# Output projection of a two-layer hybrid block: the loads of y are moved into strands of their own

## The chip, the cores and the metric

One core of one Trainium2 chip runs the whole program. Its metric is the device time of one execution in microseconds (us). TensorE (PE in the profile; PEld is its loading of weights) multiplies matrices, VectorE (DVE), ScalarE (ACT) and GpSimd (POOL) work on elements, and SyncE (SP) issues the DMAs that move data between device memory and the on-chip buffers. Each engine runs its own list of instructions in order and waits on semaphores for the others. SPq is SyncE's queue of DMA issues.

## The reference, cut to what matters

The reference is two layers of a bidirectional block over 256 context tokens and 1024 latent tokens of width 1024. In each layer four mixers (mLSTM, differential attention, GLA, gated DeltaNet) give 256 columns of y each. The part that is changed here is the end of a layer:

```
yx = jnp.concatenate([o[1] for o in outs], axis=-1)
x = x + gt[:, None, :] * (yx @ w_out[l])
if need_ctx:
    yc = jnp.concatenate([o[0] for o in outs], axis=-1)
    ctx = ctx + gt_c * (yc @ w_out[l])
```

Layer 0 does this for all ten tiles of 128 tokens, layer 1 for the eight latent tiles alone.

## The kernel before, in words

**The planner.** The program is not written in the order in which it runs. Its parts are strands (`Strand`, line 132), each a Python function in a thread of its own, of which one runs at a time. `Issue` (line 141) keeps a clock for each engine and for SyncE's DMAs ("D"), and a table of when each buffer was last written and read. When a strand wants to issue an instruction, `__call__` (line 310) works out from which moment its operands are there (`dep`) and what it will cost. A DMA counts 0.475 us on SyncE's clock (line 369); its data counts as landed 0.65 us after the issue plus its bytes at 360 GB/s behind the transfers before it, plus 1.0 us (lines 392 to 394). `choose` (line 256) then lets the strand go that can start first; of strands that compete for one engine the one with the smaller rank wins (`RANK`, line 34: "first turn" 1, "out turn" 2, "mlstm" 1). `spawn` (line 229) adds a strand, `need` (line 298) parks one until another has called `set` (line 306) with that name. These names order the writing of the program; what the engines really wait for are semaphores on buffers. All of the kernel's instructions carry the line of the planner's call, L406, in the profile, so groups are told apart by tile names.

**Buffers.** `Pool` (line 441) gives tiles by tag with a number of buffers. A new tile in an old buffer waits until that buffer's last readers are through.

**Output projection in two groups.** The 1024 rows of w_out are cut into eight blocks of 128, and y's columns likewise. `out_first` (line 2651) takes blocks 2, 3, 6, 7 (attention and DeltaNet), which are ready early, and writes x plus its share to the buffer xp in device memory. It runs while the end of GLA and the mLSTM are still at work. `outproj` (line 2729) takes blocks 0, 1, 4, 5 (mLSTM and GLA) and adds them to xp. `q_.need((l, "out first"))` (line 2744) sets it behind the first group. The text calls these the first and the second group.

For each tile of tokens a group does the following:

- `out_load` (line 2611) loads the tile of y, 128 x 512 f32 (262,144 bytes), into one of two buffers tagged "y";
- `out_turn` (line 2624) makes four transposes on TensorE into a PSUM tile "tr", a copy by ScalarE and a subtraction by VectorE into yT, the two halves of a split of y; each has two buffers;
- `out_product` (line 2636) makes 12 products of 128 x 512 for each of the two halves of the columns (nh), 24 in all, into a PSUM tile "o" with two buffers;
- VectorE multiplies by the gate row gtb and adds x or the partial sum (`evacs`, line 2692; `finishes`, line 2850), and a DMA stores the result.

Before the change one strand, `turns` (line 2682 and line 2753), does the load and the turn of a tile one behind the other. For tile i it waits until the products of tile i-2 have been issued, loads y, and turns it. The products are in the strand that spawns the others (lines 2717 and 2885). In `finishes` the load of x for tile i+1 needs `(l, "yT", i + 1)` (line 2855), and the gate row is loaded behind it (line 2865); there are two gate rows in layer 0, one for the context tiles and one for the latent tiles. In layer 0 four more strands (`norms`, `late_turns`, `splits`, `loads`, lines 2783 to 2848) norm and transpose the finished rows for layer 1.

In layer 0 the first group's loads of y are issued from 1043.8 to 1155.5 us and the second's from 1193.3 to 1286.5 us, in layer 1 from 2198.6 to 2308.6 and from 2340.0 to 2382.9 us.

Of the kernel before, what the change touches and what calls it, by code (L numbers as in the profile page):

```python
# [33 lines left out]
RANK = {"evac": 2, "weights": 3, "mlstm": 1, "first": 2, "finish": 2, "proj": 4, "qk": 2, "ahead": 1, "behind": 2, "inner": 0, "gla gates": 2, "decays": 1,  # L34
        "states": 0, "att pe": 1, "att norm": 2, "first turn": 1, "out turn": 2, "out": 4, "mod": 0}
# [105 lines left out]
class Issue:  # L141
# [161 lines left out]
                self.give()  # L303
                self.me.wait = None

    def set(self, name):
        self.done.add(name)


    def __call__(self, e, op, fn, a, k):  # L310
# [119 lines left out]
def _build(tc, nc, A, out, root, dbg):  # L430
    q_ = Issue()
# [34 lines left out]
    def mark(label):  # L466
        if q_.me:
            q_.me.label = label

    def dma(dst, src):  # L470
        SP.dma_start(out=dst, in_=src)
# [2120 lines left out]
    def out_factors(L, p):  # L2592

        l = L.l
        lam_init = 0.8 - 0.6 * math.exp(-0.3 * l)
        fac = (0.25, 0.5 * (1.0 - lam_init), 0.5, 0.5)
        wcol = p([128, 8], "wcol")
        for g in range(4):
            V.tensor_scalar(wcol[:, 2 * g:2 * g + 2], pc(l, ("wn", "wn1", "wn2", "wn3")[g], 0, 2), fac[g], None, ALU.mult)
        return wcol  # L2600
# [10 lines left out]
    def out_load(L, t, ks, op):  # L2611

        b = Box()
        b.t, b.v = t, 1 if t < NCT else 0
        b.y = op([128, len(ks), 128], "y", 2)
        if len(ks) == 4:
            a = yd[L.l][128 * t:128 * t + 128, 128 * ks[0]:128 * ks[0] + 256]
            dma(b.y.rearrange("p (g c) e -> p g (c e)", c=2),
                bass.AP(a.tensor, a.offset, [a.ap[0], [128 * (ks[2] - ks[0]), 2], [1, 256]]))
        else:  # L2620
            dma(b.y.rearrange("p g c -> p (g c)"), yd[L.l][128 * t:128 * t + 128, 128 * ks[0]:128 * ks[0] + 128 * len(ks)])
        return b

    def out_turn(b, ks, op, pps):
        n = len(ks)
        b.yT = [op([128, n, 128], f"yT{i}", 2, F32R) for i in range(2)]
        for k0 in range(0, n, 4):
            m = min(4, n - k0)
            pt = pps([128, 512], "tr")
            for i in range(m):  # L2630
                P.transpose(pt[:, 128 * i:128 * i + 128], b.y[:, k0 + i, :], ident)
            pv = pt[:, :128 * m].rearrange("p (a b) -> p a b", b=128)
            S.copy(b.yT[0][:, k0:k0 + m], pv)
            V.tensor_tensor(b.yT[1][:, k0:k0 + m], pv, b.yT[0][:, k0:k0 + m], ALU.subtract)
# [16 lines left out]
    def out_first(L, wp, end):  # L2651


        l, ks = L.l, (2, 3, 6, 7)
        mark(f"{l}out.first")
        q_.need((l, "w", end, 3))
        raws, wo, O = {}, {}, Box()

        def raw(i):
            if i < len(ks):  # L2660
                raws[i] = wp([128, DM], "wr", 2)
                dma(raws[i], A["w_out"][l, 128 * ks[i]:128 * ks[i] + 128, :])
        raw(0)
        raw(1)
        wcol = out_factors(L, wp)
        for i, (k, name) in enumerate(zip(ks, ((l, "block", end - 1), (l, "half", end), (l, "block", end), (l, "ml")))):
            q_.need(name)
            if i == 3:
                q_.need((l, "levels"))
                O.st = ExitStack()  # L2670
                O.p, O.ps = Pool(O.st, "of"), Pool(O.st, "ofps", PSUM)
                wo[k] = out_split(raws.pop(i), wcol[:, k:k + 1], lambda j, nh: O.p([128, 512], f"wo{j}{nh}", dt=F32R))
            else:
                wo[k] = out_split(raws.pop(i), wcol[:, k:k + 1], lambda j, nh: wp([128, 512], f"w{j}", 6, F32R))
            raw(i + 2)
        q_.need((l, "gdn"))
        bs, n = {}, range(len(L.yt))

        def ev(*k):
            return (l, "of", *k)  # L2680

        def turns():
            mark(f"{l}out.first")
            for i in n:
                if i > 1:
                    q_.need(ev("p", i - 2, 1))
                bs[i] = out_load(L, L.yt[i], ks, O.p)
                out_turn(bs[i], ks, O.p, O.ps)
                bs[i].ps = {}
                q_.set(ev("yT", i))  # L2690

        def evacs():
            mark(f"{l}out.first")
            gtb = {}
            xs = {}

            def load(i):
                xs[i] = O.p([128, DM], "st", 2)
                dma(xs[i], xin(l, L.yt[i]))
            load(0)  # L2700
            for i in n:
                if i + 1 < len(n):
                    load(i + 1)
                t = L.yt[i]
                gt = gates_of(L, t, O.p, gtb)
                for nh in range(2):
                    cs = slice(512 * nh, 512 * nh + 512)
                    q_.need(ev("p", i, nh))
                    ps = bs[i].ps[nh]
                    V.tensor_tensor(ps, ps, gt[:, cs], ALU.mult)  # L2710
                    V.tensor_tensor(xs[i][:, cs], ps, xs[i][:, cs], ALU.add)
                    q_.set(ev("e", i, nh))
                dma(xp[l][128 * t:128 * t + 128, :], xs[i])
                q_.set((l, "first", t))
        q_.spawn(RANK["first turn"], turns)
        q_.spawn(RANK["first turn"], evacs)
        for i in n:
            q_.need(ev("yT", i))
            for nh in range(2):
                if i:  # L2720
                    q_.need(ev("e", i - 1, nh))
                ps = bs[i].ps[nh] = O.ps([128, 512], "o", 2)
                out_product(bs[i], wo, ks, ps, nh)
                q_.set(ev("p", i, nh))
        q_.need((l, "first", L.yt[-1]))
        O.st.close()
        q_.set((l, "out first"))

    def outproj(L):

        l, full = L.l, L.full
        mark(f"{l}out")
        two = parts == "magd"
        ks = (0, 1, 4, 5) if two else tuple(range(8))
        with ExitStack() as st:
            wp, op = Pool(st, "wo", side="right"), None
# [8 lines left out]
            op = Pool(st, "op", side="right")  # L2745
            pps = Pool(st, "opps", PSUM, "right")
# [3 lines left out]
            n = len(L.yt)  # L2750
            todo = [None] * n

            def turns():
                mark(f"{l}out.turn")
                for i in range(n):
                    if "m" in parts:
                        q_.need((l, "mlstm", i))
                    if i > 1:
                        q_.need((l, "o", i - 2, 1))
                    todo[i] = out_load(L, L.yt[i], ks, op)  # L2760
                    todo[i].i, todo[i].ps = i, {}
                    out_turn(todo[i], ks, op, pps)
                    q_.set((l, "yT", i))
                q_.set((l, "turns"))

            def place(t):
                g = next(g for g, (t0, n_) in enumerate(GRP) if t0 <= t < t0 + n_)
# [3 lines left out]
            def ev(*k):  # L2771
                return (l, "late", *k)
            xts, parts_, there = {}, {}, set()
# [76 lines left out]
            def finishes():  # L2850
                mark(f"{l}out.fin")

                def load(i):
                    t = L.yt[i]
                    q_.need((l, "yT", i), (l, "first", t))
                    if i > 2 and not end:
                        q_.need(ev("t", i - 3))
                    x = todo[i].x = op([128, DM], "x", 3)
                    dma(x, xp[l][128 * t:128 * t + 128, :])
                load(0)  # L2860
                for i, t in enumerate(L.yt):
                    if i + 1 < n:
                        load(i + 1)
                    b = todo[i]
                    gt = gates_of(L, t, op, gtb)
                    for nh in range(2):
                        cs = slice(512 * nh, 512 * nh + 512)
                        q_.need((l, "o", i, nh))
                        ps = b.ps[nh]
                        V.tensor_tensor(ps, ps, gt[:, cs], ALU.mult)  # L2870
                        V.tensor_tensor(b.x[:, cs], ps, b.x[:, cs], ALU.add)
                        q_.set((l, "fin", i, nh))
                    if last:
                        dma(out[0, 128 * (t - NCT):128 * (t - NCT) + 128, :], b.x)
                    else:
                        dma(x1[t], b.x)
                    q_.set((l, "fins", i))
            q_.spawn(RANK["out turn"], turns)
            q_.spawn(RANK["out turn"], finishes)
            if end:  # L2880
                q_.set((l, "late"))
# [54 lines left out]
```

## Time and profile before

| | |
|---|---|
| median of 3 runs | 2408.47 us (2407.11 to 2413.15) |
| the profiled execution, its own time | 2405.2 us |
| its span, first to last instruction | 2403.3 us |
| TensorE busy / weight loads | 2113.9 us (88%) / 1737.7 us (72%) |
| VectorE, ScalarE, GpSimd busy | 1500.8, 981.6, 834.4 us |
| granted TensorE clock, mean | 0.942 of full speed |
| DMA on SyncE's queue | 331.69 MB, 46.1% of 16 engines |
| loads of y for the output projection | 36 of 256 KB |

Busy time is the time in which an engine runs instructions; the idle time before an instruction is put down to what released it. A row of the timeline merges neighbours of one kind: start, length, engine, operation, output tile <- input tiles, shapes, count, and in brackets the idle time ahead of it with its releaser. An issue on SPq lasts as long as SyncE needs to hand the DMA over; the transfer ends later. A stretch's DMA share is the mean busy share of the 16 DMA engines, worked out from the times of packets, so that a full stretch can read a little over 1. The granted clock is the share of full speed at which TensorE was allowed to run.

### The profile page before, as it was taken

How to read it: one execution, taken by the hardware profiler on the slowest of the kernel's cores; microseconds unless marked ns; L12 is line 12 of the kernel's file. 1: busy time of each engine (PE TensorE's matmuls, PEld its weight loads, DVE VectorE, ACT ScalarE, POOL GpSimd, SP SyncE). 2: the span in 40 equal slices, each digit the busy share in tenths (PEclk: the TensorE clock that was granted, in tenths of full speed). 3: DMA queues.
4: the chain of work that ended last, by engine and by line, in shares of the span. 5: the costliest groups of instructions: out<-in, count | busy, mean ns of one | idle time of the engine just before them, and what ended most of it. 6: DMA issues, size and time to landing. Idle time of an engine off the chain costs nothing. (4 is left out here: it accounts for less than half of the span.)

```text
span 2403.3 us, 57716 instructions
## 1 busy us (share of the span) xinstructions
PE 2113.9 (88%) x23367; PEld 1737.7 (72%) x23367; DVE 1500.8 (62%) x2726; ACT 981.6 (41%) x2168; POOL 834.4 (35%) x1048
## 2 busy tenths in 40 slices
PE   5898999999898998888877888889999889976888
PEld 1656778888776677876765668888788667775776
DVE  3586669555386863537666476696633778655475
ACT  2346412433276763213334264313322667632240
POOL 1244523555122224332431244433433122255240
PEclk7899999999999999989989899999999999986999
DMA  7347643445513116258963236433444431164595
GB/s 264 108 140 233 192 147 102 146 146 161 161 44 93 53 51 166 67 128 252 280 214 114 70 108 189 135 113 100 144 124 125 120 98 35 50 170 99 155 302 184
DMA packets 348053, 335.38 MB, mean 140 GB/s; under 512 B 93147, under 2 KB 292283, under 8 KB 347275
## 3 DMA queue, kind: packets, MB, share of 16 engines
q1 hardware_dynamic: 347786, 331.69, 46.1%
q8 instruction: 185, 3.03, 0.5%
q14 instruction: 82, 0.66, 0.1%
HBM read 226.78 MB, written 107.43 MB: 139 GB/s over the span
## 5 line engine op out<-in xcount | busy, mean ns | idle before, releaser
L406 PE MATMUL mm<-w,hT 128*128 128x256 f32 x4512 | 641.2, 293 | 17.6 <-DVE st L406 10.2
L406 PEld LDWEIGHTS mm<-w,hT 128*128 128x128 f32 x4512 | 576.1, 193 | 50.4 <-issue 20.5
L406 PE MATMUL mm<-hT,w 128*128 128x512 f32 (+1 forms) x1680 | 388.8, 377 | 20.3 <-ACT w L406 5.9
L406 PEld LDWEIGHTS mm<-hT,w 128*128 128x128 f32 x1680 | 283.2, 194 | 91.9 <-issue 20.8
L406 DVE TENSOR_REDUCE st<-sc 128x1 f32<-128x1024 f32 (+1 forms) x200 | 200.0, 1026 | 66.8 <-PE sc L406 65.6
L406 ACT ACTIVATE p<-sc,st 128x256 f32<-128x256 f32 (+1 forms) x272 | 211.3, 786 | 68.3 <-DVE st L406 51.7
L406 POOL TENSOR_TENSOR w<-wr,w 128x512 fp32r<-128x512 f32 x54 | 80.7, 1495 | 275.3 <-ACT w L406 220.9
L406 POOL TENSOR_TENSOR hss<-hss,mhalf 128x2 f32<-128x2 f32 (+2 forms) x72 | 104.1, 1446 | 157.1 <-DVE hss L406 143.1
L406 PE MATMUL o<-wo,yT 128*128 128x512 f32 x540 | 148.9, 412 | 4.8 <-DVE x L406 3.2
L406 PE MATMUL sc<-KT,qt 96*128 96x512 f32 (+1 forms) x400 | 124.2, 400 | 29.8 <-DMA KT<-akh 12.9
L406 ACT COPY wt<-tr 128x512 f32<-128x512 f32 (+1 forms) x200 | 102.2, 511 | 66.0 <-PE tr L406 65.6
L406 ACT COPY st<-mm 128x512 f32<-128x512 f32 (+1 forms) x81 | 44.9, 554 | 204.2 <-PE mm L406 142.0
L406 POOL TENSOR_TENSOR ss<-ss,mhalf 128x1 f32<-128x1 f32 (+1 forms) x39 | 68.4, 1754 | 168.9 <-DVE ss L406 168.7
L406 PEld LDWEIGHTS o<-wo,yT 128*128 128x128 f32 x540 | 102.1, 195 | 29.6 <-DVE x L406 3.8
L406 PE MATMUL tr<-k_ident,p 128*128 128x128 f32 x656 | 115.2, 281 | 7.5 <-ACT wt L406 7.0
L406 POOL TENSOR_TENSOR st<-st 128x1 f32<-128x1 f32 (+1 forms) x136 | 27.1, 199 | 270.8 <-ACT p L406 190.4
L406 ACT CAST w<-wr 128x512 fp32r<-128x512 f32 x128 | 77.4, 622 | 98.0 <-PE mm L406 56.7
L406 PE MATMUL po<-wt,av 128*64 128x128 f32 x1312 | 105.3, 284 | 3.5 <-DVE aacc L406 3.5
L406 PEld LDWEIGHTS sc<-KT,qt 96*128 96x128 f32 x400 | 63.6, 196 | 58.9 <-ACT p L406 30.9
L406 DVE SCALAR_TENSOR_TENSOR p<-p,st,p 128x1280 f32<-128x1280 f32 (+1 forms) x72 | 103.0, 1430 | 2.5 <-POOL st L406 2.3
L406 PE MATMUL o<-w,yT 128*128 128x512 f32 x324 | 100.9, 439 | 4.0 <-DVE st L406 4.0
L406 DVE TENSOR_TENSOR w<-wr,w 128x512 fp32r<-128x512 f32 x74 | 68.1, 922 | 54.5 <-ACT w L406 54.3
(314 smaller groups left out, 4062.8 us busy)
## 6 DMA issues: line engine op xcount, KB each, us to landing
wr<-in_w_in SPq DMA_DIRECT2D x64, 512.0 KB
wm<-in_w_mod SPq DMA_DIRECT2D x64, 256.0 KB
y<-y SPq DMA_DIRECT2D x36, 256.0 KB
xp<-st SPq DMA_DIRECT2D x18, 512.0 KB
pd<-rs_NG SPq DMA_DIRECT2D x18, 512.0 KB
kq<-kq SPq DMA_DIRECT2D x18, 512.0 KB
x<-xp SPq DMA_DIRECT2D x18, 512.0 KB
wm<-in_w_mod SPq DMA_DIRECT2D x16, 512.0 KB
```

The costliest lines, as they stand in the source:

```text
L406: r = fn(*a, **k)
```

## The change

In both groups the load leaves `turns` for a new strand `fetches`, spawned ahead of `turns` with the same rank. `fetches` loads tile i as soon as the transposes of tile i-2 have been issued ("turned"), which are the last readers of its buffer. `turns` waits for the load ("y") and, as before, for the products of tile i-2. In the second group the wait for the mLSTM's tile moves with the load. `set` takes several names, so that one call can set "turned" and "yT".

```diff
-    def set(self, name):
-        self.done.add(name)
+    def set(self, *names):
+        self.done.update(names)
...
         def turns():
             mark(f"{l}out.first")
             for i in n:
+                q_.need(ev("y", i))
                 if i > 1:
                     q_.need(ev("p", i - 2, 1))
+                out_turn(bs[i], ks, O.p, O.ps)
+                q_.set(ev("turned", i), ev("yT", i))
+
+        def fetches():
+            mark(f"{l}out.first")
+            for i in n:
+                if i > 1:
+                    q_.need(ev("turned", i - 2))
                 bs[i] = out_load(L, L.yt[i], ks, O.p)
-                out_turn(bs[i], ks, O.p, O.ps)
                 bs[i].ps = {}
-                q_.set(ev("yT", i))
+                q_.set(ev("y", i))
...
+        q_.spawn(RANK["first turn"], fetches)
         q_.spawn(RANK["first turn"], turns)
...
             def turns():
                 mark(f"{l}out.turn")
                 for i in range(n):
+                    q_.need((l, "y there", i))
+                    if i > 1:
+                        q_.need((l, "o", i - 2, 1))
+                    out_turn(todo[i], ks, op, pps)
+                    q_.set((l, "y turned", i), (l, "yT", i))
+                q_.set((l, "turns"))
+
+            def fetches():
+                mark(f"{l}out.turn")
+                for i in range(n):
                     if "m" in parts:
                         q_.need((l, "mlstm", i))
                     if i > 1:
-                        q_.need((l, "o", i - 2, 1))
+                        q_.need((l, "y turned", i - 2))
                     todo[i] = out_load(L, L.yt[i], ks, op)
                     todo[i].i, todo[i].ps = i, {}
-                    out_turn(todo[i], ks, op, pps)
-                    q_.set((l, "yT", i))
-                q_.set((l, "turns"))
+                    q_.set((l, "y there", i))
...
+            q_.spawn(RANK["out turn"], fetches)
             q_.spawn(RANK["out turn"], turns)
```

## Rows read from the trace of the kernel before

**Rows 1.** The page: busy time of each engine, its share of the span, instructions.

```profile
PE 2113.9 (88%) x23367; PEld 1737.7 (72%) x23367; DVE 1500.8 (62%) x2726; ACT 981.6 (41%) x2168; POOL 834.4 (35%) x1048
```

**Rows 2.** TensorE's waits, 1040–1200, 1190–1300, 2240–2403: us, times, longest.

```profile
PE tr L406 <- DMA y<-y: 4.1, 3, 3.2
...
PE tr L406 <- DMA y<-y: 7.2, 5, 3.2
...
PE tr L406 <- DMA y<-y: 8.5, 4, 5.8
```

**Rows 3.** Busy time by stretch (windows); columns in the first line.

```profile
core 0: us, PE busy (x) PEld busy (x) DVE busy (x) ACT busy (x) POOL busy (x), PEclk, DMA share, GB/s
1193.00:1256.00 63.00, 48.30 (x233) 38.32 (x232) 39.27 (x76) 23.02 (x55) 24.60 (x25) 0.85 0.69 224
1330.00:2198.00 868.00, 780.02 (x9026) 663.09 (x9029) 554.07 (x964) 388.11 (x825) 310.82 (x403) 0.94 0.38 112
2254.00:2340.00 86.00, 72.93 (x604) 62.71 (x594) 57.09 (x120) 31.77 (x97) 36.91 (x45) 0.92 1.02 284
2357.00:2390.00 33.00, 33.00 (x153) 26.73 (x153) 18.38 (x28) 2.93 (x5) 0.00 (x0) 1.00 0.63 214
```

**Rows 4.** Timeline of SyncE's queue, layer 0, second group.

```profile
1223.51 0.85 SPq L406 DMA_DIRECT2D y<-y  x1
...
1230.99 0.82 SPq L406 DMA_DIRECT2D y<-y  x1
1234.21 0.34 SPq L406 DMA_DIRECT2D x<-xp  x1
1234.61 0.45 SPq L406 DMA_DIRECT2D gtb<-gt  x1
```

**Rows 5.** Timeline of TensorE, same stretch: start, us, what, [idle before <-releaser].

```profile
1207.66 0.66 PE L406 MATMUL tr<-k_ident,y 128*128 128x128 f32 x4 [0.96 <-DMA y<-y]
...
1219.21 9.93 PE L406 MATMUL o<-wo,yT 128*128 128x512 f32 x36
...
1233.12 0.63 PE L406 MATMUL tr<-k_ident,y 128*128 128x128 f32 x4 [0.40 <-DMA y<-y]
...
1238.31 0.63 PE L406 MATMUL tr<-k_ident,y 128*128 128x128 f32 x4 [3.19 <-DMA y<-y]
1240.32 1.09 PE L406 MATMUL tr<-k_ident,x 128*128 128x128 f32 x4 [1.38 <-DVE x L406]
1244.01 5.96 PE L406 MATMUL o<-wo,yT 128*128 128x512 f32 x14 [2.61 <-DVE x L406]
```

**Rows 6.** Timeline of TensorE, layer 0, first group, tile 0.

```profile
1046.93 1.12 PE L406 MATMUL tr<-k_ident,y 128*128 128x128 f32 x4 [3.18 <-DMA y<-y]
```

**Rows 7.** Timeline of TensorE, layer 1, both groups.

```profile
2247.90 0.38 PE L406 MATMUL tr<-k_ident,y 128*128 128x128 f32 x2
...
2280.08 1.09 PE L406 MATMUL tr<-k_ident,y 128*128 128x128 f32 x4 [5.78 <-DMA y<-y]
...
2349.52 0.63 PE L406 MATMUL tr<-k_ident,y 128*128 128x128 f32 x4 [1.48 <-DMA y<-y]
...
2355.67 0.63 PE L406 MATMUL tr<-k_ident,y 128*128 128x128 f32 x4 [1.78 <-DVE o L406]
```

**Rows 8.** Timeline of SyncE's queue, layer 1, first group, tiles 3 and 4.

```profile
2253.87 0.53 SPq L406 DMA_DIRECT2D y<-y  x1
...
2274.74 0.56 SPq L406 DMA_DIRECT2D y<-y  x1
```

**Rows 9.** The chain that ended last, layer 1: start, us, what.

```profile
2274.74 5.20 DMA y<-y
...
2347.94 6.91 DMA gtb<-gt
```

**Rows 10.** SyncE's waits, 1040–1200: us in total, times, longest.

```profile
SPq L406 <- DVE st L406: 10.1, 4, 6.0
SPq L406 <- DMA xp<-st: 8.0, 5, 2.3
```


## The prediction, made before the changed kernel was run

> **What bounds the kernel now.** I read the page's busy shares first, then the windows by stretch, then what TensorE waits for, then single loads on the SyncE queue. TensorE is busy for 88% of the span [rows 1], so over the whole run only idle TensorE time can be won, and the question is how much of it is owed to y. For each of the 36 y tiles TensorE makes four transposes and 24 products. It sat idle before transposes of y for 4.1 us in layer 0's first group, 7.2 us in its second group and 8.5 us in both groups of layer 1 [rows 2]. Together that is 19.8 us in 12 waits, 0.8% of the run: a ceiling for what waiting on y costs directly, unless something stands behind a late y as well.
>
> The stretches differ. In the first half of layer 0's second group TensorE is busy 48.30 of 63 us with the DMA engines at 0.69. While layer 1's first group shares the chip with the mLSTM, TensorE is busy 72.93 of 86 us and the DMA share is 1.02: there the transfers themselves press. In layer 1's last stretch TensorE is busy for 33.00 of 33 us, although y is issued there tile by tile too [rows 3]. So nothing is to be had at the very end: one tile's 24 products cover the load there.
>
> **Where y is late.** In layer 0's second group, tile 3's load went out at 1223.51 and tile 4's at 1230.99 [rows 4]; their transposes began at 1233.12 and 1238.31 after idle 0.40 and 3.19 us [rows 5]. From issue to use that is 9.6 and 7.3 us. Tile 4's products are further back: 36 products took 9.93 us [rows 5], so 24 take about 6.6 us. That is less than the load. More hangs on tile 3: line 2855 lets the finishing strand load x for tile 3, and after it the second gate row, only when the planner has seen tile 3's turn. Both went out at 1234.21 and 1234.61 [rows 4], and the products of tile 3 then waited 2.61 us for VectorE's finishing of tile 2 [rows 5].
>
> **The change, part by part.** The number of DMAs, matmuls and copies stays as it is; nothing is added on an engine. What moves is the place of 32 of the 36 loads in SyncE's queue: from behind the second product of tile i-2 to behind the transposes of tile i-2, which is a product of 24 earlier; tile 1's load goes out beside tile 0's. Only the first two loads of a group are free of any wait. The transposes of tile i still wait for the products of tile i-2 (two yT buffers), so they cannot themselves move ahead without limit. `set` taking several names costs the chip nothing: it runs while the program is written.
>
> *Layer 0, the first group.* Of the 4.1 us, 3.18 us stand before tile 0 [rows 6], whose load isn't moved. That leaves 0.9 us. Bounds 0 to -0.9; I take -0.3, since the DMA share of this stage soon comes to that of layer 1.
>
> *Layer 0, the second group.* The five waits of 7.2 us [rows 2] go if y is there: tile 3's load would stand behind the transposes of tile 1 at 1207.66 instead of at 1223.51 [rows 4, 5], some 15 us earlier against 9.6 us of flight. Tile 3 could then turn when tile 1's products end, at about 1219.21 + 24/36 x 9.93 = 1225.8 rather than 1233.12, and x and the gate row would follow up to 7 us earlier, so at best the 2.61 us go too: -9.8. What is late next is VectorE's norm and finish of the tile before: the same stretch has TensorE waiting 1.38 and 2.61 us for it [rows 5]. If such waits return in full (4.0 us), -3.2 is left. I take -5, nearer to the lower end, as VectorE's norms (39.27 us busy of 63 [rows 3]) are not moved.
>
> *Layer 1, the first group.* One wait of 5.78 us, before tile 4, makes up most of it [rows 7]; the four waits of both groups sum to 8.5 us [rows 2], and 1.48 us of those are the second group's [rows 7]. So 7.0 us at best. Tile 3's and tile 4's loads left at 2253.87 and 2274.74 [rows 8]; tile 4's would follow the transposes of tile 2, which end at 2248.3 [rows 7], before the DMA engines fill. The chain that ended last passes through this load for 5.20 us [rows 9]. But the DMA share of 1.02 at 284 GB/s [rows 3] says that after it the mLSTM's own loads set the pace: if so only two loads of 262,144 bytes leave the full stretch, 0.92 us each by that rate, -1.8. Between -1.8 and -7.0 I take -3.5, as the chain turns to other DMAs later.
>
> *Layer 1, the second group.* Tile 1's 1.48 us, then 1.78 us behind the finishing of tile 0 [rows 7], which waited for the gate row (6.91 us on the chain [rows 9]). Bounds 0 to -3.3; I take -1.5, tile 1's wait. Once the dense stretch begins, nothing: the cover is the 24 products of a tile, at 33.00 of 33 us [rows 3].
>
> *The price on SyncE's queue.* At each of four group starts a second load goes ahead of x, the gate row and the mLSTM's loads: 0.53 to 0.85 us of issue [rows 4, 8] and 0.92 us of transfer by the rate above, at most some 1.5 us each or 6 in all; below nothing it cannot be. I take +0.5, because at three of the four starts nothing waits for what follows.
>
> *The planner.* Every strand after 1043 us is re-ordered by the planner's clock, layer 1's middle too. The trace cannot price that; TensorE idles 868 - 780 = 88 us between 1330 and 2198 [rows 3], and I let a twentieth of it come or go: +-4.4, taken as 0.
>
> The sum is -0.3 - 5 - 3.5 - 1.5 + 0.5 = **-9.8 us**, bounds -25.4 to +5.4. It is made against the profiled execution (2405.2 us, span 2403.3), which lies 3.3 us below the median of the three runs shown, 2408.47 us. I carry it over to the median: **2398.7 us**. A measurement of this kernel can tell about 0.3%, 7.2 us, from no change.
>
> A rule against the change: the Trainium skill, "DMA: Bandwidth & Descriptors", section on the anatomy of one DMA, gives (for GpSimd-issued transfers) about 2.0 us fixed plus bytes at 436 GB/s; an estimate from it is 2.6 us for a y tile, which 24 products cover, and the sum would be 0. The measured 7.3 and 9.6 us [rows 4, 5] speak against it here, as SyncE's transfers share full engines, so the rows decide.
>
> **The rivals.** *The DMA engines are the bound* (0.30). Then layer 1's first group gives 1.8, layer 0's second group 3.2, the rest nothing: -5 + 0.5 = -4.5, about **2404 us**. For it speaks the share of 1.02 [rows 3]; against it the 5.78 us hole, in which TensorE stood for this one load [rows 7].
>
> *SyncE blocks on the new waits* (0.14), **slower**. A load that is issued behind transposes waits on SyncE until they have run, and every load of the mLSTM behind it waits along. SyncE now loses 10.1 us in 4 waits for evacuations and 8.0 us in 5 for stores in layer 0's first group [rows 10], 2.0 us each. Nine y loads lie in the two full stretches: 18 us lost, and layer 1's 3.5 us not won: -6.3 + 18 = +11.7, **2420 us**. It decides from about 1.1 us lost for each. Against it: TensorE runs these transposes early, and in full stretches the queue is behind the plan anyway, so that waits have passed. The Trainium skill, the same page and section, says that semaphore waits happen on the issuing sequencer before dispatch; by that rule the blocking is possible, and the waits of rows 10 agree that SyncE waits in order.
>
> *A larger gain* (0.13). TensorE's granted clock averages 0.85 between 1193 and 1256 us [rows 3], so part of it ran at 1.2 instead of 2.4 GHz after idle spells. If the holes close and the stretch runs at 1.00, 48.30 x 0.15 = 7.2 us come on top: -17, **2391.5 us**.
>
> *The change does not do what it says* (0.03): the planner sets the loads where they were. **2408.5 us**.
>
> **How the numbers follow.** The forecast itself, -7.2 to -14 us, has 0.40; its own range is 2394 to 2401. Faster by over 0.3%: 0.40 + 0.13 = 0.53. Within: 0.30 + 0.03 = 0.33. Slower: 0.14. The range goes from 2385 (larger gain with the planner's swing) to 2414 (the bounds' upper end), which leaves out most of the blocking case and the far lower end.
>
> **What would show it.** Right: y waits of TensorE down from 19.8 us to the 3.18 us of tile 0 and little more; layer 0's x load and gate row for tile 3 several us sooner after the group's start; the hole before tile 4 in layer 1 gone; the last dense stretch as long as before. Wrong: SyncE waiting for transposes for over 10 us in the full stretches; or y waits gone and TensorE idle as long, for the mLSTM's loads or VectorE's norms. A swing of over 5 us between 1330 and 2198 would mean that the planner, not the loads, set the result.

## The result, and the profile after

The changed kernel takes 2438.09 us, the median of 3 runs (2436.53 to 2442.72), against 2408.47 us before: ratio 1.0111, 95% interval 1.0069 to 1.0153. It is slower by 1.1% by that ratio, some 27 us (the two medians lie 29.6 us apart), and lies above the range of the prediction. The span of its profiled execution is 2436.3 us, 33.0 us longer than before.

The page's busy shares answer to [rows 1]:

```profile
PE 2130.2 (87%) x23367; PEld 1750.1 (72%) x23367; DVE 1504.5 (62%) x2720; ACT 985.3 (40%) x2169; POOL 833.7 (34%) x1055
```

The same 23367 matmuls keep TensorE busy for 16 us more; the other 17 us of the span are idle time of TensorE. The mean granted clock of the execution is 0.935, and 0.942 before; an estimate from these, 2113.9 x 0.942 / 0.935 = 2129.7 us, is close to the 2130.2 us of busy time, so the 16 us go with the lower clock.

TensorE's waits for y, in layer 0's first group, its second group and layer 1's groups (1040 to 1205, 1200 to 1330, 2200 to 2436 us; us in total, times, longest), answer to [rows 2]:

```profile
PE tr L406 <- DMA y<-y: 2.9, 1, 2.9
...
PE tr L406 <- DMA y<-y: 5.1, 1, 5.1
...
PE tr L406 <- DMA y<-y: 0.8, 1, 0.8
```

They fell from 19.8 us in 12 waits to 8.8 us in 3: the loads are early, as the change means them to be. Layer 1's hole of 5.78 us before tile 4 [rows 7] is gone. And yet the kernel is slower.

Windows set to the stretches of [rows 3] (layer 0's second group, layer 1's middle, the mLSTM with the first group, the dense last stretch; columns as there). The new order has moved matmuls from one to another (406 for 604 in the third line), so the shares can be compared and not the lengths:

```profile
1206.00:1269.00 63.00, 46.04 (x213) 37.98 (x212) 32.98 (x65) 22.40 (x48) 19.58 (x19) 0.78 0.66 211
1343.00:2221.00 878.00, 779.64 (x8917) 662.14 (x8915) 561.15 (x960) 388.06 (x819) 312.32 (x405) 0.94 0.37 111
2301.00:2390.00 89.00, 73.58 (x406) 63.59 (x407) 56.19 (x124) 33.00 (x102) 34.50 (x47) 0.87 0.96 272
2395.00:2428.00 33.00, 33.00 (x153) 26.77 (x152) 18.30 (x28) 2.94 (x5) 0.00 (x0) 1.00 0.59 206
```

The dense last stretch is as it was, 33.00 us of 33. The other stretches are no denser: layer 1's middle, in which no load of y is issued, is busy for 0.89 of its window, where it was 0.90.

To see where the time went, I read four landmarks from SyncE's queue: the first load of y in layer 0, the first load of layer 1's gate weights (graw), the first load of y in layer 1, and the last store of the output; between the last two stands the mLSTM's first load of NG (pd<-rs_NG), which opens its output part. The timeline of the queue, after:

```profile
1044.68 0.57 SPq L406 DMA_DIRECT2D y<-y  x1
...
1330.79 1.64 SPq L406 DMA_DIRECT2D graw<-in_w_in  x3
...
2224.68 1.21 SPq L406 DMA_DIRECT2D y<-y  x2
...
2301.48 0.59 SPq L406 DMA_DIRECT2D pd<-rs_NG  x1
...
2426.64 5.93 SPq L406 DMA_DIRECT2D out<-x  x2
```

Before, the same landmarks stand at 1043.83, 1317.92, 2198.64 and 2394.02 us. In us between them:

| stage | before | after | difference |
|---|---|---|---|
| layer 0's two groups (first y to graw) | 274.1 | 286.1 | +12.0 |
| layer 1's middle (graw to its first y) | 880.7 | 893.9 | +13.2 |
| layer 1's two groups (first y to last store) | 195.4 | 202.0 | +6.6 |

So all stages lose, and the largest part is lost where the change does nothing. Between these landmarks the matmuls are nearly the same, so busy time can be compared; first before, then after:

```profile
1043.83:1317.92 274.09, 219.69 (x1552) 173.92 (x1552) 167.46 (x344) 93.77 (x233) 86.97 (x101) 0.91 0.71 210
1317.92:2198.64 880.72, 785.42 (x9066) 666.84 (x9068) 557.01 (x975) 391.70 (x832) 314.73 (x408) 0.94 0.38 111
2198.64:2394.02 195.38, 165.71 (x1644) 136.47 (x1645) 122.28 (x237) 48.34 (x139) 57.86 (x66) 0.92 0.72 211
```

```profile
1044.68:1330.79 286.11, 226.71 (x1554) 181.68 (x1552) 162.30 (x338) 97.33 (x240) 86.12 (x101) 0.87 0.70 201
1330.79:2224.68 893.89, 787.68 (x9057) 667.80 (x9057) 565.61 (x975) 391.99 (x827) 317.65 (x414) 0.94 0.37 109
2224.68:2426.64 201.96, 171.88 (x1649) 140.54 (x1650) 121.13 (x237) 48.24 (x138) 56.14 (x67) 0.91 0.69 204
```

Of the 31.8 us, 15.4 are busy time of TensorE (7.0, 2.3 and 6.2 us by stage) and 16.3 are idle time (5.0, 10.9 and 0.4 us). The mean granted clock fell most in layer 0's groups, from 0.91 to 0.87. Whether it fell because of new holes between the matmuls is not shown. (Two profiles of one order can differ by 10 us in these stages, as e9 shows below, so the split is rough.)

In layer 1's groups the mLSTM's first load of NG now goes out 76.8 us behind the first load of y, 56.5 us before. Ahead of it stands a wait of the kind that a rival named:

```profile
2240.73 0.41 SPq L406 DMA_DIRECT2D mv<-mv  x1
2256.44 0.53 SPq L406 DMA_DIRECT2D y<-y  x1
2258.38 0.34 SPq L406 DMA_DIRECT2D xp<-st  x1
...
2261.41 0.43 SPq L406 DMA_DIRECT2D kq<-kq  x1
...
2267.64 2.35 SPq L406 DMA_DIRECT2D y<-hy  x4
```

Between 2241.1 and 2256.4 us SyncE waits with tile 3's load until the transposes of tile 1 have read the buffer; the mLSTM's loads kq and GLA's loads gz stand behind it. Whether this wait is what puts the mLSTM back is for e3 to tell. Over the whole run SyncE waits for transposes for 101.9 us (42.7 before):

```profile
SPq L406 <- PE tr L406: 101.9, 28, 15.2
```

Two readings offered themselves: SyncE's blocking (theory queue, later loads), or the new order in which the planner sets everything behind the first changed strand (theory replan, later order).

### The profile page after: what moved, and what is told of

Read it like the earlier page. It is cut to its first block, busy times and chain, and to the rows that moved or that the text cites. A ratio compares the mean times of both kernels' runs of the same rounds, so it can differ in the third digit from the quotient of the medians.

```text
span 2436.3 us, 57725 instructions
## 1 busy us (share of the span) xinstructions
PE 2130.2 (87%) x23367; PEld 1750.1 (72%) x23367; DVE 1504.5 (62%) x2720; ACT 985.3 (40%) x2169; POOL 833.7 (34%) x1055
## 4 chain that ended last, share of the span: by engine, by line
PE 54%; DMA 14%; DVE 11%; issue 7%; ACT 5%; SPq 5%; POOL 3%; POOLq 0%; ACTq 0%; DVEq 0%
PE mm L406 24%; PE po L406 5%; SPq L406 5%; PE o L406 5%; PE tr L406 4%; PE sc L406 3%; PE pd L406 3%; PE p L406 3%; DMA wm<-in_w_mod 2%; DMA wr<-in_w_in 2%; DVE st L406 2%; DMA pd<-rs_NG 2%; PE mod L406 1%; PE puw L406 1%; ACT p L406 1%
## 5 line engine op out<-in xcount | busy, mean ns | idle before, releaser
L406 ACT CAST w<-wr 128x512 fp32r<-128x512 f32 x128 | 76.8, 621 | 104.2 <-DMA wr<-in_w_in 55.2
L406 PEld LDWEIGHTS sc<-KT,qt 96*128 96x128 f32 x400 | 62.9, 195 | 60.2 <-ACT p L406 32.1
L406 PEld LDWEIGHTS tr<-k_ident,p 128*128 128x128 f32 x656 | 75.5, 141 | 35.3 <-ACT wt L406 20.7
```

The costliest lines, as they stand in the source:

```text
L406: r = fn(*a, **k)
```

## The experiments

They ran on four chips (e1 to e4, e5 to e8, e9 to e11 and e12 to e15 on one each), on which the kernel before has medians of 2419 to 2422 us; every ratio is against runs of before beside it on the same chip, with its 95% interval.

**Order and place taken apart.** A DMA's entry in the planner's clock was split from its issue. In e1 the planner counts each load where before had it, so that all four compute engines have exactly the order of before, while the real load is issued behind the transposes of tile i-2 (tiles 0 and 1 at the group's start; in the second group only where the mLSTM's tile is there by then, else at the old place). In e2 it is the other way round: the order of the changed kernel, the loads late.

```diff
+    def out_count(b):          # planner's clock only
+        q_("D", "dma_start", lambda **k: None, (), b.io)
+    def out_issue(b):          # the real DMA, no clock
+        nc.sync.dma_start(**b.io)
...
-                bs[i] = out_load(L, L.yt[i], ks, O.p)
+                out_count(bs[i])
                 out_turn(bs[i], ks, O.p, O.ps)
+                early(i + 2)   # tile and out_issue
```

> The order of every instruction on TensorE, VectorE, ScalarE and GpSimd is that of before; only the loads of y are moved in SyncE's queue, to right behind the transposes of tile i-2. Theory queue (SyncE stands behind a load of y whose buffer is still to be read by transposes, and the loads behind it start late): slower than before by 10 to 35 us, 2418 to 2443 us, with SyncE waiting for transposes for 20 us or more in layer 1's first group, and the mLSTM's first load of NG in layer 1 30 us or more later after the first load of y than the 56.5 us of before. Theory replan (the new order of the other work costs the time, and early loads are good in themselves): 2395 to 2408 us.

e1: 2423.04 us, ratio **1.0011** (0.9994 to 1.0029). Neither theory's number came: early loads in the old order are neither slower nor faster. TensorE's waits for y, over the whole run, are gone; the kernel before, run again on another of these chips (e9, below), has

```profile
PE tr L406 <- DMA y<-y: 23.5, 12, 5.9
```

and e1 has none. SyncE waits for transposes for 62.9 us in e1 (the second line is of the loads issued past the planner, line 2625):

```profile
SPq L406 <- PE tr L406: 37.6, 12, 12.7
...
SPq L2625 <- PE tr L406: 25.3, 10, 7.8
```

against this in e9:

```profile
SPq L406 <- PE tr L406: 41.2, 15, 11.6
```

So 21.7 us more of blocking and 23.5 us less of waiting for y together move the time by no more than 0.3% (7 us). Whether the two cancel is for e4 to tell. What took the place of the waits is in TensorE's waits of layer 1's groups (2200 to 2430 us), first e9, then e1:

```profile
PE tr L406 <- DMA y<-y: 9.3, 4, 5.9
PE m L406 <- ACT cs L406: 8.5, 1, 8.5
...
PE m L406 <- POOL wb L406: 2.4, 2, 1.4
```

```profile
PE m L406 <- ACT cs L406: 8.5, 1, 8.5
PE m L406 <- POOL wb L406: 8.2, 4, 3.3
PE o L406 <- DVE x L406: 4.2, 1, 4.2
```

9.3 us for y went, and 5.8 us more for GpSimd's product with wb and 4.2 us for VectorE's finishing came: TensorE arrives earlier at the next thing that is late.

> The order of every instruction on the four compute engines is that of the changed kernel; only the loads of y go back behind the products of tile i-2, just ahead of the transposes that read them. Theory queue: the blocking is gone, so most of the 30 us is won back: 2403 to 2418 us. Theory replan: the order holds the loss, 2430 to 2450 us.

e2: 2505.37 us, **1.0345** (1.0317 to 1.0373). Neither theory's number came: without the early loads the new order does not win back its loss, it loses more. The run is harsher than its expectation says, and so no clean test of theory queue: this order has the transposes planned right behind the products, and TensorE waits for a late load 22 times:

```profile
PE tr L406 <- DMA y<-y: 70.3, 22, 7.5
```

It tells that the new order rests on early loads, not what the order costs by itself. That is read from e1 against the changed kernel: both have early loads, and 1.0011 against 1.0111 is the new order's, with the blocking that comes with it. The next run takes the blocking out.

**Three buffers.** `b.y = op([128, len(ks), 128], "y", 3)` in the changed kernel. The order of the compute engines stays (in the traces VectorE's differs in 4 of 2720 rows, ScalarE's and GpSimd's in none), the blocking goes.

> The changed kernel with three buffers for y instead of two, so that a load waits for the transposes of tile i-3, which are a tile older. Theory queue: SyncE hardly waits for transposes, 2400 to 2415 us. Theory replan: the order is about that of the changed kernel, 2425 to 2445 us.

e3: 2440.50 us, **1.0083** (1.0061 to 1.0105). SyncE's wait for transposes is down to the level of before,

```profile
SPq L406 <- PE tr L406: 43.5, 16, 11.7
```

and the loss remains. If blocking has a share in the changed kernel's 1.0111, it is some 0.3%, and the intervals overlap. By stage nothing is won:

```profile
1050.93:1336.40 285.47, 225.94 (x1552) 181.47 (x1552) 163.44 (x337) 97.46 (x240) 85.12 (x101) 0.87 0.69 201
1336.40:2229.91 893.51, 789.66 (x9062) 670.79 (x9062) 563.65 (x975) 391.72 (x827) 318.30 (x414) 0.93 0.37 109
2229.91:2432.57 202.66, 173.90 (x1649) 141.84 (x1645) 122.66 (x237) 48.38 (x138) 56.05 (x67) 0.89 0.70 203
```

The three stages are as long as in the changed kernel, within 0.7 us each. In layer 1 SyncE waits for transposes for 3.7 us between the first load of y and the mLSTM's first load of NG (23.4 us in the changed kernel), and still that load goes out 76.9 us behind. So it is the order that puts the mLSTM back, not the blocking.

**One tile ahead in the old order.** As e1, with three buffers, and tile i+1 loaded where before loads tile i.

> Order of the compute engines as before, three buffers for y, and each load where before had the load of the tile ahead of it: one tile early, into a buffer that was read long ago. Theory queue: early loads without the wait, so the 16 us of waits before transposes of y go and something of it is kept: 2395 to 2405 us. Theory replan: the same, 2395 to 2405 us. If it is not faster than before, then the waits for y were covered by others, as the rival says in which the DMA engines set the pace: 2405 to 2412 us.

e4: 2418.93 us, **0.9992** (0.9973 to 1.0010). TensorE's waits for y are down to 0.9 us and SyncE's for transposes are 41.6 us, as in e9; the time is that of before. So the saved waits are worth at most 0.3% by themselves and nothing that was measured, and in e1 there was no gain of that size that the blocking could have eaten: both are covered. This is the mildest form of the change, and no run of this study is clearly faster than the kernel before.

**Is it the mLSTM's place?** Counted in TensorE's order, 72 products of layer 1's first group stand ahead of the mLSTM's first weighing before, 114 after. e5 holds that group back:

```diff
                 if i > 1:
                     q_.need(ev("turned", i - 2))
+                    if l:
+                        q_.need((l, "m states"))   # set behind the mLSTM's last state_out
```

> The changed kernel, with the load of the third and later tiles of layer 1's first group held until the mLSTM's states of that layer have been written. The planned order then has 66 products of that group ahead of the mLSTM's first weighing (before: 72, changed: 114). Theory order (the planner lets the first group's products go ahead of the mLSTM, whose loads fill the DMA engines and set the end): the 20 to 25 us of layer 1's end come back, so +2 to +14 us against before. Theory loads (early loads of y cost in themselves): no change against the changed kernel, +20 to +32 us.

e5: 2458.01 us, **1.0152** (1.0132 to 1.0173). Neither theory's number came. The run is slower still, with 66 products ahead; but in its trace the mLSTM's first load of NG goes out 74.0 us behind the first load of y all the same, so holding the group back did not bring the mLSTM forward, and e5 does not settle the question. e13 and e15 below do.

**Parts of the change.** e6 has the new strands in the second group only, e15 in the first only, e10 in layer 0 only, e11 in layer 1 only.

> The change in the second group only; the first group loads as before, in both layers. The planned order has 120 products of layer 1's first group ahead of the mLSTM's first weighing all the same, since the planner's clock differs from layer 0's second group on. Theory order: +15 to +30 us against before, though that group's loads are not moved. Theory loads: the first group is as before, so within 8 us of before.

> The change in the first group only, in both layers. 1415 rows of TensorE's order differ, 120 products ahead of the mLSTM's first weighing. Theory order: +15 to +35 us, like the whole change and like the second group alone, not a share of it. Theory loads: the two groups share the loss, so +0 to +10 us beside the +25 us of the second group alone.

> The change in layer 0 alone (both groups); layer 1 loads y as before. The planner plans all that follows anew: 1349 rows of TensorE's order differ from before. Theory order: nearly the whole loss is here, +20 to +32 us, of it 8 us or more in layer 1's middle and end, where no load was moved. Theory loads: the part of layer 0 alone, +8 to +14 us, and layer 1 as long as before.

> The change in layer 1 alone. Everything up to layer 1's first group is ordered as before, and behind it the order differs little: 105 rows of TensorE's order. Theory order: within 6 us of before, with most of layer 1's 8.5 us of waits for y gone. Theory loads: the share of layer 1's sixteen tiles, +8 us or more, with SyncE waiting for transposes.

e6: 2446.54 us, **1.0119** (1.0101 to 1.0138). e15: 2429.21 us, **1.0033** (1.0013 to 1.0053). e10: 2454.22 us, **1.0124** (1.0103 to 1.0145). e11: 2425.05 us, **1.0022** (1.0004 to 1.0041). e6 and e11 came as theory order expected, e10 (+35 us) lost more than either theory said. The parts do not add up: the second group alone costs as much as both, layer 0 alone as much as both layers. e11, whose order is nearly that of before, costs almost nothing, although TensorE's waits for y are shorter there too (17.6 us, 23.5 in e9). e15's number (+10 us) lies below what theory order expected and at the upper end of what theory loads did; it has 120 products ahead of the mLSTM, whose first load of NG goes out 81.2 us behind the first load of y, and that this costs so little speaks against the mLSTM's place. Theory loads falls with e6, which was to stay within 8 us, and with the runs that follow.

**A new order with no load moved.** The kernel before, with one line that sets the planner's DMA clock on by a little where layer 0's first group starts:

```diff
         def turns():
             mark(f"{l}out.first")
+            if l == 0:
+                q_.now["D"] += 1.0
```

> The kernel before, with no load moved; only the planner's clock for DMAs is set on by 1.0 us where layer 0's first group starts, so that it plans another order. 115 products stand ahead of the mLSTM's first weighing in layer 1. Theory order: +12 to +30 us against before. Theory loads: no load was moved, so within 6 us of before.

> As the last, with 2.0 us. 93 products stand ahead of the mLSTM's first weighing in layer 1. Theory order: between before and the last, +4 to +16 us. Theory loads: within 6 us of before.

> The kernel before, no load moved, the planner's clock for DMAs set on by 0.05 us where layer 0's first group starts. 1410 rows of TensorE's order differ from before. Theory order at large (any new plan is some per mille longer, since before's order is a good one among many): +15 to +40 us, as with 1 and 2 us. Theory size (a small disturbance gives a small loss): within 5 us of before.

> As the last, with 0.1 us. 900 rows differ, but in layer 1 the first group and the mLSTM stand to each other as before: 72 products ahead of the mLSTM's first weighing. Theory layer 1's end (that place makes the loss): within 5 us of before. Theory order at large: +10 to +40 us.

> As the last two, with 0.5 us: 1583 rows differ, 120 products stand ahead of the mLSTM's first weighing in layer 1. Both theories of the order: +15 to +40 us.

| run | clock set on by | median us | ratio | 95% interval |
|---|---|---|---|---|
| e12 | 0.05 us | 2426.11 | 1.0020 | 1.0001 to 1.0038 |
| e13 | 0.1 us | 2440.18 | 1.0075 | 1.0047 to 1.0104 |
| e14 | 0.5 us | 2440.62 | 1.0081 | 1.0051 to 1.0110 |
| e7 | 1.0 us | 2457.26 | 1.0161 | 1.0142 to 1.0179 |
| e8 | 2.0 us | 2441.80 | 1.0085 | 1.0051 to 1.0119 |

The chip does the same work in these kernels, with the same loads from the same strands; only the plan is another. A plan is the order and, for some copies and products, the choice of the engine, which helpers make by the planner's clocks (`evac`, `sub`, `mulv`, lines 473 to 497): e12 has 2707 instructions on VectorE and 1061 on GpSimd, before 2726 and 1048. They lose 0.2 to 1.6%, and the changed kernel's 1.1% lies in the midst of them. e13 keeps the mLSTM's place (72 products ahead) and loses 0.75%: theory layer 1's end falls. e7 (+36 us) and e8 (+21 us) lost more than was expected of them, and e12 (+7 us) less, so a new order is not always dear. The landmarks show where e13 loses; first e9, then e13:

```profile
1056.56 0.57 SPq L406 DMA_DIRECT2D y<-y  x1
...
1335.90 1.74 SPq L406 DMA_DIRECT2D graw<-in_w_in  x3
...
2219.34 0.56 SPq L406 DMA_DIRECT2D y<-y  x1
...
2417.09 5.94 SPq L406 DMA_DIRECT2D out<-x  x2
```

```profile
1047.50 0.57 SPq L406 DMA_DIRECT2D y<-y  x1
...
1323.89 1.75 SPq L406 DMA_DIRECT2D graw<-in_w_in  x3
...
2231.24 0.55 SPq L406 DMA_DIRECT2D y<-y  x1
...
2429.43 5.94 SPq L406 DMA_DIRECT2D out<-x  x2
```

Layer 0's groups take 279.3 us in e9 and 276.4 in e13, layer 1's groups 197.8 and 198.2, but layer 1's middle 883.4 and 907.4. There e13's matmuls keep TensorE busy for 13.2 us more and leave it idle for 10.7 us more; again first e9, then e13:

```profile
1335.90:2219.34 883.44, 787.07 (x9066) 667.85 (x9068) 558.82 (x975) 391.74 (x832) 312.49 (x408) 0.93 0.38 110
1323.89:2231.24 907.35, 800.26 (x9066) 677.57 (x9068) 548.50 (x973) 391.45 (x830) 320.17 (x412) 0.92 0.37 107
```

The largest single wait of TensorE that e13 has there and e9 has not is for a load of the DeltaNet's gate rows (1330 to 1900 us):

```profile
PE tr L406 <- DMA pk<-rs_BH: 8.4, 1, 8.4
```

Each order loses in places of its own: e10 and e14 lose most in layer 1's groups, which take 211.7 and 214.7 us, 197.8 in e9.

The lower clock is no matter of one profile. Averaged over all runs of a kernel, the granted clock is 0.937 to 0.939 in before and in e1, e4, e9, e11, e12 and e15, whose ratios are at most 1.0033; it is 0.930 to 0.934 in e3, e5 to e8, e10 and e13, whose ratios are 1.0075 to 1.0161, and 0.923 in e2. Only e14 (0.937, 1.0081) stands outside. So in these runs a dear order goes with matmuls that run at a lower clock, beside any longer idle time; which of the two comes first is not shown.

**The kernel before again.**

> The kernel before itself, unchanged: ratio 0.998 to 1.002 by every theory. It gives a trace of before on the chip on which these runs are made, so that the stages can be compared on one chip.

e9: 2422.47 us, **1.0005** (0.9989 to 1.0022), as expected. Its profile is 10 us longer from the first load of y to the last store than the profile of before in [rows 3], though the order is the same (5 us of it busy time of TensorE), so differences of a few us between single profiles say little; the ratios carry the verdicts.

## Why the prediction was wrong, point by point

**The step that failed is the planner's term**, "I let a twentieth of it come or go: +-4.4, taken as 0". The five clock shifts, which move nothing but the plan, measured it: +0.2 to +1.6%, that is +5 to +39 us, never below 0. Nothing in the trace stood behind the twentieth, so a term of up to 39 us was left beside a sum of -9.8, and it was wrongly taken as even to both sides. It was also priced on the wrong thing: on TensorE's idle time in layer 1's middle alone. Of the 31.8 us that the changed kernel's three stages lose, 10.9 are such idle time; 15.4 are the matmuls' own time at a lower granted clock, for which the sum has no term, and 5.4 are idle time in the output projection's own stages. Eleven orders other than that of before were timed (the changed kernel, e5 to e8, e10 to e15), and none was faster. That the order of before is a good one among many is what they suggest; they are too few to say how good. The prediction's own test was right: a swing of over 5 us in layer 1's middle "would mean that the planner, not the loads, set the result", and it was +13.2 (+2.7 in e9, whose order is that of before).

**The gains (-0.3, -5, -3.5, -1.5)** failed as well, in a second way. Each counted a wait of TensorE for y as time won, with a share given back. e1 took all of these waits away, 23.5 us, and the time moved by +0.1% (-0.1 to +0.3). The share given back is the whole: the sum of these terms, by itself, is 0 within 7 us. (The second term also counted on an earlier x and gate row, which e1 does not move; see below for these.) The rival that said so for the full stretches (the DMA engines set the pace) was right about the outcome there; that transfers were the cover is not shown, since what replaced the waits in layer 1 was GpSimd and VectorE. The estimate from the Trainium skill's page "DMA: Bandwidth & Descriptors", anatomy of one DMA, came to a sum of 0 too, but by a load of 2.6 us (its fit is for GpSimd-issued transfers), which the measured loads of 7.3 and 9.6 us [rows 4, 5] contradict.

**SyncE blocks on the new waits**: this rival said slower, 2420 us, and slower it came, but by another cause, so its sign was right by luck. The blocking is there, 101.9 us against 42.7, and once 15.2 us long. With three buffers it is gone, 0.8% of 1.1% stays and no stage is shorter by more than 0.7 us; in the old order 62.9 us of it cost nothing that can be measured. By the two ratios it has about a quarter of the loss, and with their intervals perhaps none. The place was wrong too: the longest wait fell ahead of the full stretch, at the end of GLA.

**The gate row of layer 0's second group** was to go out up to 7 us sooner after the group's start: it went from 41.3 us (1193.34 to 1234.61) to 37.8 us (1206.04 to 1243.86), 3.5 us, and the group's stage was not shorter for it.

**The dense last stretch** stayed as long as it was, as predicted. **The larger gain** by TensorE's clock did not come: the granted clock of layer 0's second group is 0.78 after, 0.85 before [rows 3]. The rival looked at the right quantity, but it went the other way.

What stays open: which pairs of instructions make one order dearer than another, and whether the lower clock is cause or result of the longer idle time. The mLSTM's place falls with e13 (72 products ahead as before, +0.75%) and e15 (120 ahead, +0.33%); no other single place was tried.

## What to carry to other kernels

Where a planner orders the whole program, a change to one of its inputs is two changes: the edit itself and a new order of all that follows, and the second can be the larger, as here; measure it by an edit that moves the planner and nothing else, and measure the first by moving the instruction with the planner's account left as it was. Do both before you believe that a local idea is bad or good. A wait that is named in the profile is worth only the distance to the next thing that is late, and in e1 and e4 that distance was nothing that could be measured. Compare the busy time of equal work as well as the waits: 15.4 us of the 31.8 us between the two profiles were in it.

## What was not expected of the hardware

TensorE's waits for one stream of loads went from 23.5 us to 0 and the time stayed within 0.3% (e1), and to 0.9 us with the time within 0.3% (e4). SyncE stood for 62.9 us in all behind transposes, 21.7 us more than in e9, without a measurable loss (e1). With nothing but another plan, as many matmuls kept TensorE busy for 13.2 us more in layer 1's middle of e13, at a mean granted clock of 0.92 (0.93 in e9).
